# A hybrid decoder layer on one core: the first head's row maxima turned in the projection's stage and loaded with the queries, and a third score pass of 100 rows

## The chip, the core and the metric

The kernel is one launch on one core of a Trainium2 chip. The core has five engines with queues of their own: TensorE (PE, matmuls; PEld are its weight loads), VectorE (DVE), ScalarE (ACT), GpSimd (POOL) and SyncE (SP, which here issues nearly all DMAs). Each engine works through its instructions in order and waits at semaphores for the others. Operands lie in SBUF (128 partitions), matmul results in the eight banks of PSUM, the rest in DRAM. The metric is the device time of one execution in microseconds (us); the figure for a kernel is the median over its runs.

## The reference, cut to what matters

One layer over 1040 tokens (16 learned meta tokens ahead of 1024) of width 1024: a norm, one input projection to 7328 columns, four parallel mixers, each gated and projected back, and an output projection. The change touches the second mixer, attention with 8 heads of 96 query/key dimensions (64 plain and 32 rotary) and 64 value dimensions:

```python
z = rms_norm(h_res, pre_norm_g) @ w_in
(pv, pg, cq, ckv, kr, mg, cu, cg, sbcx, sg, gl) = split_cols(z)
q = (rms_norm(cq, q_norm_g) @ w_uq) ...      # 8 heads x 96, scaled by 96 ** -0.5
kv = (rms_norm(ckv, kv_norm_g) @ w_ukv) ...  # 8 heads x (64 of k, 64 of v)
s = where(k_pos <= q_pos, q @ k.T, -inf)     # causal
p = softmax(s)                               # needs the maximum of each row of s
o = p @ v
y_b = (o * silu(mg)) @ w_out_mla
```

All of it is in float32. The output is the 1024 rows that follow the meta tokens.

## The kernel before

**Stages.** The kernel runs in three stages. In the first (up to about 641 us) PE works through the input projection: pairs of 256-column chunks, each made of seven products of twelve matmuls each (128x512 most of them), into the banks ps_pa to ps_pd. The other parts (convolutions, norms, the queries and keys, and weights made ready for later) are written as Python generators, the lanes, which are advanced a step after each product. Results go to DRAM (z, th, q, k, kr, v). In the second stage (to about 841 us) PE does the attention, head by head and for each head two halves c of 512 queries, with the projections of the other mixers (ps_y) as fill. The third is the projection of attention's result and the output projection.

**Order.** No engine's order is written by hand. Every operation is recorded with its reads and writes (`Plan.record`), and `Plan.flush` then plays the recorded list through a rough model of the engines' times and issues the instructions in the order in which that model starts them. So an edit in one place can move instructions elsewhere. It flushes once per stage. All compute instructions are issued from one helper, so the profile calls them all L362, and they are told apart by their tiles. DMA completions of SP and ACT are counted on eight lanes (DMAHW0 to DMAHW7), which are given out in the order of issue: a DMA waits until the one eight places ahead of it has landed.

**Precision.** A float32 operand is split into a high part and the remainder (`split`), and a product is three matmuls: high x high, high x low, low x high. `q_dram` and `k_dram` hold both parts (index s of 0 and 1).

**Scores and their maxima.** For softmax the score tile is built keys by queries. Query tile `qt` and key tile `kt` have `NA = 100` partitions: 96 of data (`QK`) and four more. In the four extra rows of `kt` (high part) stands -1, loaded once from `ones_dram`; in the four extra rows of `qt` stands the row maximum of the query, each row r holding the maxima of the r-th 128 queries and zeros elsewhere. So the first of the three score passes, over 100 rows, subtracts each query's maximum within the matmul; the second and third are over 96 rows (`attend`, L1478 to L1481). Then DVE adds the causal mask on the diagonal block, ACT takes the exponential (tile p), ACT and POOL split it (tile pt), and three matmuls add it to ps_o.

**Where the maxima come from.** `row_maxima` computes scores queries by keys from the high parts alone (ps_x in the first stage, ps_s<-kt,qt in the second), masks them and reduces them on DVE to mx, and then to four columns of 128 maxima. For the first head (`h < FIRST`) this is done in the projection's stage by `task_first`, which leaves the four columns in `mrs`; for the others `maxima` does it in the attention stage, ahead of the half in which they are used. In both cases `maxima` then turns the four columns into rows: a transpose on PE (128x4 to 4x128, into a ps_s bank), and one DVE operation that multiplies it by the unit matrix into the four extra rows of `qt`.

**The switch from stage one to two.** The second stage's first loads are issued on SP while PE is still in the projection: `load_q(0, 0)`, the masks, the -1 rows and a zero fill of `vs`, then head 0's keys and values (`load_kv(0)`: kt<-k, kt<-kr twice, vs<-v three times, vt<-v), the queries of (0, 1) and (1, 0), and head 1's keys and values. The first head's first score matmul needs `qt` with its maxima and `kt`.

Of the kernel before, what the change touches and what calls it, by code (L numbers as in the profile page):

```python
# [21 lines left out]
F32 = mybir.dt.float32  # L22
F32R = mybir.dt.float32r
BF16 = mybir.dt.bfloat16
AF = mybir.ActivationFunctionType
ALU = mybir.AluOpType
AX = mybir.AxisListType
# [3 lines left out]
P = 128  # L31
# [3 lines left out]
L = NT + NM  # L35
# [7 lines left out]
QK = 96  # L43
# [7 lines left out]
FIRST = 1  # L51
# [21 lines left out]
def f(ap):  # L73
    return ap.bitcast(F32)
# [393 lines left out]
def trunk_kernel(ctx, tc, a):  # L468
    nc = tc.nc
    plan = Plan(nc)  # L470
    PE, ACT, DVE, POOL, SP = (plan.engine(e) for e in ("PE", "ACT", "DVE", "POOL", "SP"))
# [7 lines left out]
    def ld(out, in_):  # L479
        SP.dma_start(f(out) if out.dtype == F32R else out, f(in_) if in_.dtype == F32R else in_)  # L480
# [17 lines left out]
    const = pool(ctx, name="const")  # L498
    dram = pool(ctx, name="dram", space=DRAM)
    ident = const.pool.tile([P, P], F32, name="ident")  # L500
# [10 lines left out]

    par = const.tile([P, NPAR + 2], F32, name="par")

    mrs = const.tile([P, FIRST, 2, 4], F32, name="mrs")

    z_dram = {}
    for n in ("a0", "a1", "ckv", "kr", "pv0", "pv1", "c0", "c1", "x0", "x1"):
        z_dram[n] = dram.tile([P, L], F32, name=f"z_{n}")
# [15 lines left out]
    mask_dram = [dram.tile([P, P], F32, name=f"mask{i}") for i in range(2)]  # L534
    zero_dram = dram.tile([NS, 2 * P], F32, name="zero")
    ones_dram = dram.tile([4, L], F32, name="ones4")

    so_dram = [dram.tile([2, P, D], F32, name=f"so{k}") for k in range(KH)]

# [13 lines left out]
    def bank(tag="x"):  # L553

        return psum.tile([P, 512], F32, tag=tag, bufs=2 if tag == "x" else 1, name=f"ps_{tag}")
# [3 lines left out]
    tp = pool(one, name="tp", reuse_waits="tile")  # L559
# [3 lines left out]
    def t4(shape, dt=F32, name="t4"):  # L563
        return tp.tile(shape, dt, tag="t4", bufs=4, name=name)
# [398 lines left out]
    def task_consts():  # L963

        for i in range(2):
            mask = w1([P, P], name="mask")
            causal(mask, 1 - 2 * i)
            ld(mask_dram[i], mask)
        t = t4([4, L], name="kone")
        POOL.memset(t, -1.0)  # L970
        ld(ones_dram, t)
        t = t4([NS, 2 * P], name="zero")
        POOL.memset(t, 0.0)
        ld(zero_dram, t)
        yield

    def k_rows(k_, h, part):
# [7 lines left out]
    def row_maxima(c, mx, q_, k_, mask, bank):  # L985

        for r in range(4):
            nk = NM + P * (4 * c + r + 1)
            nb = -(-nk // 512)
            w_ = -(-nk // nb)  # L990
            w_ += w_ % 2
            n0 = 0
            for b in range(nb):
                n = min(w_, nk - n0)
                s = bank()
                PE.matmul(s[:, :n], q_[:, P * r:P * (r + 1)], k_[:, n0:n0 + n], start=True, stop=True)
                if b == nb - 1:
                    add(DVE, s[:, n - P:n], s[:, n - P:n], mask)
                DVE.tensor_reduce(mx[:, r, b:b + 1], s[:, :n], axis=AX.X, op=ALU.max)
                n0 += n  # L1000
            yield
# [206 lines left out]
    def task_first(c):  # L1208

        n = NM + 512 * (c + 1)  # L1210
        for h in range(FIRST):
            k_ = t4([QK, L], F32R, name="k0")[:, :n]
            k_rows(k_, h, lambda x: x[:, 0, :n])
            q_ = t4([QK, 512], F32R, name="q0")
            ld(q_, q_dram[c][h][:, 0])
            mask = w1([P, P], name="mask")
            causal(mask)
            yield
            mx = tp.tile([P, 4, 3], F32, name="mx")
            POOL.memset(mx, NEG)  # L1220
            yield from row_maxima(c, mx, q_, k_, mask, bank)
            DVE.tensor_reduce(mrs[:, h, c], mx, axis=AX.X, op=ALU.max)

    def task_kv():

# [179 lines left out]
    NA = QK + 4  # L1405
    qt = {}

    def load_q(h, c):
        qt[h, c] = qk.tile([NA, 2, 512], F32R, tag="q", bufs=3, name="qt")
        ld(qt[h, c][:QK].rearrange("p s n -> p (s n)"), q_dram[c][h].rearrange("p s n -> p (s n)"))  # L1410

    load_q(0, 0)
    kt = [qk.tile([NA, 2, LK], F32R, name=f"kt{i}") for i in range(2)]
# [7 lines left out]
    for t in vs:  # L1421
        ld(t.rearrange("p c n -> p (c n)"), zero_dram)
    for t, src in ((maskS, mask_dram[0]), (maskT, mask_dram[1]),
                   *((kt[i][QK:NA, 0, :L], ones_dram) for i in range(2))):
        ld(t, src)

    def load_kv(h):
# [15 lines left out]
    def maxima(h, c):  # L1443

        q_, k_ = qt[h, c], kt[h % 2]
        if h < FIRST:
            mr = mrs[:, h, c]  # L1450
            for _ in range(4):
                yield
        else:
            mx = mxs[:, h % 2, c]
            yield from row_maxima(c, mx, q_[:QK, 0], k_[:QK, 0], maskS, lambda: bank("s"))
            mr = at.tile([P, 4], F32, tag="mr", bufs=2, name="mr")
            DVE.tensor_reduce(mr, mx, axis=AX.X, op=ALU.max)
        pm = bank("s")
        PE.transpose(pm[:4, :P], mr, ident)
        DVE.tensor_tensor(q_[QK:NA, 0, :].rearrange("p (r n) -> p r n", n=P),  # L1460
                          pm[:4, :P].unsqueeze(1).to_broadcast([4, 4, P]),
                          ident[:4, :4].unsqueeze(2).to_broadcast([4, 4, P]), op=ALU.mult)
        yield
# [3 lines left out]
    def attend(h, c):  # L1467
# [4 lines left out]
        for j in range(nj):  # L1472
# [5 lines left out]
            s = bank("s")[:kn, :n]  # L1478
            PE.matmul(s, k_[:NA, 0, ks], q_[:NA, 0, qs], start=True, stop=False)
            PE.matmul(s, k_[:QK, 0, ks], q_[:QK, 1, qs], start=False, stop=False)  # L1480
            PE.matmul(s, k_[:QK, 1, ks], q_[:QK, 0, qs], start=False, stop=True)  # L1481
            d0 = P * j - NM
            dl, dh = max(d0, 512 * c, 0), min(d0 + P, 512 * (c + 1))
            if dh > dl:
# [407 lines left out]
```

## Time and profile before

| what | value |
|---|---|
| median of 3 runs | 974.67 us (974.61 to 975.8) |
| the profiled execution: its time | 973.71 us |
| the profiled execution: its span, first to last instruction | 971.8 us |
| granted TensorE clock | 0.998 |
| PE busy | 959.1 us, 99% of the span |
| DVE, POOL, ACT busy | 695.7, 672.1, 450.7 us |
| chain of work that ended last | PE 93%, DMA 2%, DVE 2%, POOL 2%, issue 1%, ACT 1% |

The span is 1.9 us shorter than the execution's time: what lies around the instructions. In the rows of the profile, "out<-in" names the tile written and the tiles read, without buffer numbers; qt, kt, ps_s, ps_o, p and pt are the tiles named above. An "idle before" in square brackets is time in which the engine had nothing to do just before, with what ended it. Matmuls overlap, so the distance from one start to the next is what a matmul costs on PE, and the printed duration is longer. A "q" behind an engine (SPq, ACTq) is its queue: here the issue of a DMA.

### The profile page before, as it was taken

How to read it: one execution, taken by the hardware profiler on the slowest of the kernel's cores; microseconds unless marked ns; L12 is line 12 of the kernel's file. 1: busy time of each engine (PE TensorE's matmuls, PEld its weight loads, DVE VectorE, ACT ScalarE, POOL GpSimd, SP SyncE). 2: the span in 40 equal slices, each digit the busy share in tenths (PEclk: the TensorE clock that was granted, in tenths of full speed). 3: DMA queues.
4: the chain of work that ended last, by engine and by line, in shares of the span. 5: the costliest groups of instructions: out<-in, count | busy, mean ns of one | idle time of the engine just before them, and what ended most of it. 6: DMA issues, size and time to landing. Idle time of an engine off the chain costs nothing.

```text
span 971.8 us, 15351 instructions
## 1 busy us (share of the span) xinstructions
PE 959.1 (99%) x5063; PEld 817.5 (84%) x5063; DVE 695.7 (72%) x1118; ACT 450.7 (46%) x914; POOL 672.1 (69%) x623
## 2 busy tenths in 40 slices
PE   9999999999999999999999999999999999999996
PEld 9999899889888888888778888878888888788885
DVE  6946967969978985435545687346768878699956
ACT  7644333343343454554443444356465565224632
POOL 6747645566677888888679689556377696557965
PEclk9999999999999999999999999999999999999999
DMA  7145467667587686685646778699869773772644
GB/s 257 35 115 167 143 228 235 218 202 243 183 283 245 188 277 202 214 264 177 218 148 184 245 264 276 187 306 332 227 180 280 188 209 120 265 252 85 203 150 152
DMA packets 136295, 202.76 MB, mean 209 GB/s; under 512 B 20814, under 2 KB 83253, under 8 KB 135448
## 3 DMA queue, kind: packets, MB, share of 16 engines
q1 hardware_dynamic: 127240, 185.00, 61.2%
q10 hardware_dynamic: 8656, 15.74, 4.5%
q0 software_dynamic: 320, 1.05, 0.3%
q8 instruction: 40, 0.66, 0.3%
q14 instruction: 39, 0.32, 0.1%
HBM read 128.86 MB, written 72.88 MB: 208 GB/s over the span
## 4 chain that ended last, share of the span: by engine, by line
PE 93%; DMA 2%; DVE 2%; POOL 2%; issue 1%; ACT 1%; DVEq 0%; SPq 0%; POOLq 0%; ACTq 0%
PE ps_pb L362 17%; PE ps_pa L362 16%; PE ps_pc L362 15%; PE ps_o L362 9%; PE ps_u L362 8%; PE ps_pd L362 7%; PE ps_y L362 7%; PE ps_s L362 7%; PE ps_x L362 5%; PE ps_w L362 1%; DMA kt<-k 1%; POOL pt L362 1%; DMA kt<-kr 1%; POOL boM L362 0%; ACT pt L362 0%
## 5 line engine op out<-in xcount | busy, mean ns | idle before, releaser
L362 PE MATMUL ps_pb<-T,S 128*128 128x512 f32 (+2 forms) x792 | 172.4, 360 | 0.0
L362 PE MATMUL ps_pa<-B,A 128*128 128x512 f32 (+2 forms) x792 | 169.4, 359 | 0.0
L362 POOL TENSOR_TENSOR S<-ss,S 128x512 fp32r<-128x512 f32 x84 | 114.0, 1370 | 64.5 <-ACT S L362 64.3
L362 PEld LDWEIGHTS ps_pa<-B,A 128*128 128x128 f32 x792 | 134.3, 188 | 22.5 <-issue 0.7
L362 PEld LDWEIGHTS ps_pb<-T,S 128*128 128x128 f32 x792 | 134.1, 189 | 22.4 <-issue 1.0
L362 POOL TENSOR_TENSOR A<-raw,A 128x512 fp32r<-128x512 f32 x84 | 114.7, 1371 | 42.8 <-ACT A L362 40.5
L362 POOL TENSOR_TENSOR pt<-p,pt 128x512 fp32r<-128x512 f32 (+1 forms) x96 | 101.1, 1077 | 53.7 <-PE ps_s L362 25.6
L362 DVE TENSOR_TENSOR u<-ps_pb,u 128x512 f32<-128x512 f32 (+2 forms) x66 | 40.2, 610 | 80.6 <-PE ps_pb L362 76.8
L362 ACT ACTIVATE S<-ss 128x512 fp32r<-128x512 f32 x84 | 50.8, 628 | 83.9 <-DVE ss L362 52.5
L362 DVE SCALAR_TENSOR_TENSOR ps_w<-conv,par,ps_w 128x512 f32<-128x512 f32 x116 | 87.2, 752 | 2.3
L362 PE MATMUL ps_y<-bo,whl 128*128 128x512 f32 x288 | 86.2, 405 | 0.4 <-DVE th L362 0.4
L362 PE MATMUL ps_pc<-B,S 128*128 128x512 f32 (+1 forms) x396 | 86.2, 360 | 0.0
L362 PE MATMUL ps_pd<-T,A 128*128 128x512 f32 (+2 forms) x396 | 85.4, 359 | 0.0
L362 PE MATMUL ps_pc<-T,S 128*128 128x512 f32 (+1 forms) x396 | 85.0, 358 | 0.0
L362 ACT ACTIVATE p<-ps_s 128x512 f32<-128x512 f32 (+4 forms) x112 | 49.5, 443 | 59.5 <-PE ps_s L362 29.7
L362 PEld LDWEIGHTS ps_pc<-B,S 128*128 128x128 f32 x396 | 66.9, 189 | 11.7 <-issue 1.2
L362 PEld LDWEIGHTS ps_pc<-T,S 128*128 128x128 f32 x396 | 66.9, 188 | 10.7
L362 PEld LDWEIGHTS ps_pd<-T,A 128*128 128x128 f32 x396 | 66.9, 189 | 10.4
L362 PE MATMUL ps_s<-qt,kt 100*128 100x512 f32 (+4 forms) x336 | 68.0, 325 | 1.3 <-DVE qt L362 1.3
L362 PE MATMUL ps_o<-pt,vt 128*128 128x512 f32 (+7 forms) x288 | 68.1, 345 | 0.8 <-ACT ol L362 0.6
L362 PEld LDWEIGHTS ps_s<-qt,kt 100*128 100x128 f32 (+1 forms) x336 | 54.3, 176 | 11.2 <-DVE qt L362 1.6
L362 DVE TENSOR_TENSOR z<-ps_pc,u 128x512 f32<-128x512 f32 (+1 forms) x64 | 38.8, 606 | 32.7 <-PE ps_pc L362 29.0
(280 smaller groups left out, 1917.8 us busy)
## 6 DMA issues: line engine op xcount, KB each, us to landing
raw<-in_w_in_dram SPq DMA_DIRECT2D x52, 512.0 KB
th<-th SPq DMA_DIRECT2D x32, 512.0 KB
th<-z ACTq DMA_DIRECT2D x60, 256.0 KB
v<-vhl SPq DMA_DIRECT2D x16, 384.0 KB
qt<-q SPq DMA_DIRECT2D x16, 384.0 KB
vt<-v SPq DMA_DIRECT2D x8, 768.0 KB
bo<-bo SPq DMA_DIRECT2D x6, 1024.0 KB
kt<-k SPq DMA_DIRECT2D x8, 520.0 KB
```

Source lines behind the costliest of these rows:

```text
L362: getattr(self.handle[o["eng"]], o["op"])(*map(real, o["args"]), **{k: real(v) for k, v in o["kw"].items()})
```

## The change

`task_first` no longer leaves its four columns in `mrs`. It transposes them itself in the projection's stage (into a ps_x bank), copies the 4x128 result over the first four partitions of its mask tile, and writes each of the four rows by a DMA of its own into a new DRAM tile `top_dram`, which was filled with zeros beforehand, so that it holds the four extra rows of `qt` as they are to stand. `load_q` of the first head gets a second DMA that loads these four rows. In `maxima` the transposes and the DVE products of the first head's two halves are gone. Apart from this, the third score pass takes in all 100 rows, for all heads: the four extra rows of `kt`'s low part are loaded once with zeros from another new DRAM tile, so that the result stays as it was.

```diff
-    mrs = const.tile([P, FIRST, 2, 4], F32, name="mrs")
...
+    none_dram = dram.tile([4, L], F32, name="ones4")
+    top_dram = dram.tile([4, 2, 4, P], F32, name="top")
...
+        t = t4([4, L], name="knone")
+        POOL.memset(t, 0.0)
+        ld(none_dram, t)
         t = t4([NS, 2 * P], name="zero")
         POOL.memset(t, 0.0)
         ld(zero_dram, t)
+        ld(top_dram.rearrange("r c (a b) n -> (r c a) (b n)", b=2), t[:16])
...
             yield from row_maxima(c, mx, q_, k_, mask, bank)
-            DVE.tensor_reduce(mrs[:, h, c], mx, axis=AX.X, op=ALU.max)
+            mr = tp.tile([P, 4], F32, name="mr")
+            DVE.tensor_reduce(mr, mx, axis=AX.X, op=ALU.max)
+            pm = bank()
+            PE.transpose(pm[:4, :P], mr, ident)
+            DVE.tensor_copy(mask[:4].bitcast(F32R), pm[:4, :P])
+            for r in range(4):
+                ld(top_dram[r:r + 1, c, r], mask[r:r + 1])
...
         ld(qt[h, c][:QK].rearrange("p s n -> p (s n)"), q_dram[c][h].rearrange("p s n -> p (s n)"))
+        if h < FIRST:
+            ld(f(qt[h, c])[QK:NA, 0], top_dram[:, c].rearrange("r a n -> r (a n)"))
...
-                   *((kt[i][QK:NA, 0, :L], ones_dram) for i in range(2))):
+                   *((kt[i][QK:NA, 0, :L], ones_dram) for i in range(2)),
+                   *((kt[i][QK:NA, 1, :L], none_dram) for i in range(2))):
         ld(t, src)
...
         if h < FIRST:
-            mr = mrs[:, h, c]
-            for _ in range(4):
+            for _ in range(5):
                 yield
-        else:
-            mx = mxs[:, h % 2, c]
-            yield from row_maxima(c, mx, q_[:QK, 0], k_[:QK, 0], maskS, lambda: bank("s"))
-            mr = at.tile([P, 4], F32, tag="mr", bufs=2, name="mr")
-            DVE.tensor_reduce(mr, mx, axis=AX.X, op=ALU.max)
+            return
+        mx = mxs[:, h % 2, c]
+        yield from row_maxima(c, mx, q_[:QK, 0], k_[:QK, 0], maskS, lambda: bank("s"))
+        mr = at.tile([P, 4], F32, tag="mr", bufs=2, name="mr")
+        DVE.tensor_reduce(mr, mx, axis=AX.X, op=ALU.max)
...
-            PE.matmul(s, k_[:QK, 1, ks], q_[:QK, 0, qs], start=False, stop=True)
+            PE.matmul(s, k_[:NA, 1, ks], q_[:NA, 0, qs], start=False, stop=True)
```

Instructions move at three places: the last 100 us of the projection, where the maxima are computed, the switch of stages, and the first 30 us of the attention. Ahead of the first and behind the last of them each engine's order is what it was.

PE at the switch, before. The rows run from the last product of the projection into the first half of head 0 (ps_s<-qt,kt: the score passes, three for each block of keys, kt_6897 being head 0's keys and kt_6903 head 1's; ps_s<-kt,qt: row maxima of head 1):

```order
L362 MATMUL ps_pc<-B_320,S_6687 128x512 x9
L362 MATMUL ps_s<-ident,mrs 4x128 x2
L362 MATMUL ps_s<-qt,kt_6897 128x512 [waits DMAHW3_49,DMAHW2_49,DMAHW5_49,DMAHW1_49,DVE_49]
L362 MATMUL ps_s<-qt,kt_6897 128x512 x2
...
L362 MATMUL ps_s<-qt,kt_6897 16x16 x2
L362 MATMUL ps_s<-kt_6903,qt 128x144 [waits DMAHW3_49,DMAHW2_49,DMAHW4_49,DMAHW1_49,Activation_49]
L362 MATMUL ps_o<-pt,vt_6911 128x512 [waits DMAHW7_49,Activation_49]
L362 MATMUL ps_s<-qt,kt_6897 128x512 [waits DMAHW0_49,Activation_49]
```

The same place after the change (kt_6922 is head 0's keys, kt_6924 head 1's):

```order
L362 MATMUL ps_pc<-B_320,S_6708 128x512 x9
L362 MATMUL ps_s<-qt,kt_6922 128x512 [waits DMAHW5_49,DMAHW6_49,DMAHW4_49,DMAHW7_49,DMAHW2_49,DMAHW0_49]
L362 MATMUL ps_s<-qt,kt_6922 128x512
L362 MATMUL ps_s<-qt,kt_6922 128x512 [waits DMAHW4_49]
...
L362 MATMUL ps_s<-qt,kt_6922 16x16 x2
L362 MATMUL ps_s<-qt,kt_6922 128x512 [waits DMAHW6_49,DMAHW5_49,Activation_49]
L362 MATMUL ps_s<-qt,kt_6922 128x512 x2
L362 MATMUL ps_o<-pt,vt_6934 128x512 [waits DMAHW4_49,Activation_49]
L362 MATMUL ps_s<-qt,kt_6922 128x512 [waits Activation_49]
...
L362 MATMUL ps_o<-pt,vt_6934 128x400
L362 MATMUL ps_s<-kt_6924,qt 128x144 [waits DMAHW2_49,DMAHW1_49,DMAHW7_49,DMAHW0_49,Activation_49]
```

The two transposes and the wait for DVE are gone from the first score matmul, which now waits for loads alone; three score matmuls of the second half stand ahead of the first ps_o, and head 1's first maxima stand eleven matmuls later.

SP at the switch, before: the second stage's loads, from the first head's queries to head 1's keys:

```order
L362 DMA qt<-q_4075 96x1024 [waits DMAHW2_49]
L362 DMA maskS<-mask_5675 128x128 [waits DMAHW3_49]
L362 DMA maskT<-mask_5777 128x128 [waits DMAHW4_49]
L362 DMA kt_6897<-ones_5875 4x1040 [waits DMAHW6_49,DMAHW5_49,DMAHW1_49]
L362 DMA vs_6899<-zero 80x256 [waits DMAHW0_49,DMAHW6_49,DVE_49,Pool_49]
L362 DMA vs_6901<-zero 80x256 [waits DMAHW7_49]
L362 DMA kt_6903<-ones_5875 4x1040 [waits DMAHW0_49,PE_49]
L362 DMA kt_6897<-k_1678 64x2x1040 [waits DMAHW1_49]
...
L362 DMA qt<-q_5254 96x1024 [waits DMAHW0_49]
L362 DMA qt<-q_4075 96x1024 [waits DMAHW1_49]
L362 DMA kt_6903<-k_1678 64x2x1040 [waits DMAHW2_49]
```

And after (qt<-top are the four rows of maxima; the kt<-ones_5885 are the zeros):

```order
L362 DMA qt<-top 4x512 [waits DMAHW5_49]
...
L362 DMA vs_6920<-zero 80x256 [waits DMAHW1_49,DMAHW2_49,DVE_49,Pool_49]
L362 DMA kt_6922<-ones_5872 4x1040 [waits DMAHW2_49]
L362 DMA kt_6924<-ones_5872 4x1040 [waits DMAHW3_49,PE_49]
L362 DMA kt_6922<-ones_5885 4x1040 [waits DMAHW4_49]
L362 DMA kt_6924<-ones_5885 4x1040 [waits DMAHW5_49]
L362 DMA kt_6922<-k_1678 64x2x1040 [waits DMAHW6_49]
...
L362 DMA qt<-q_5254 96x1024 [waits DMAHW5_49]
L362 DMA qt<-top 4x512 [waits DMAHW6_49]
L362 DMA qt<-q_4075 96x1024 [waits DMAHW7_49]
L362 DMA kt_6924<-k_1678 64x2x1040 [waits DMAHW0_49]
```

Three more small loads stand ahead of head 0's keys and four ahead of head 1's. The place eight behind the projection's last store from ACT (th<-z), which head 0's keys had, is now that of the second -1 rows, three places ahead of the keys.

PE in the projection after the change, where the first half's maxima end (ps_x<-k_5925,q_5944 are the row maxima, mr the four columns; T, B, S are operands of the projection). Before, the transpose's row was not there and the product ran on:

```order
L362 MATMUL ps_x<-k_5925,q_5944 128x264
L362 MATMUL ps_pb<-T_291,S_5932 128x512 x6
L362 MATMUL ps_x<-ident,mr 4x128
L362 MATMUL ps_pb<-T_291,S_5932 128x512
L362 MATMUL ps_x<-k_5950,q_5985 128x328
```

The transpose stands six matmuls behind the last of the scores whose maxima it turns; that of the second half stands seven behind.

## The prediction

> **What bounds the kernel now.** I read the page's first lines, then PE's waits, then stages, then the place of the one wait that the change removes.
>
> ```profile
> PE 959.1 (99%) x5063; PEld 817.5 (84%) x5063; DVE 695.7 (72%) x1118; ACT 450.7 (46%) x914; POOL 672.1 (69%) x623
> PE 93%; DMA 2%; DVE 2%; POOL 2%; issue 1%; ACT 1%; DVEq 0%; SPq 0%; POOLq 0%; ACTq 0%
> ```
>
> PE bounds the whole span: 959.1 of 971.8 us, and 93% of the chain that ended last. So only two things count: work put on PE or taken from it, and time in which PE stands. Of its waits, one stands at the place of the change:
>
> ```profile
> PE ps_s L362 <- DVE qt L362: 1.3, 1, 1.3
> ```
>
> It is one wait of 1.3 us for DVE's writing of `qt`. The windows round the switch of stages give its place (columns: busy time of PE, PEld, DVE, ACT, POOL with counts, clock, DMA share, GB/s):
>
> ```profile
> 627.00:641.00 14.00, 14.00 (x64) 11.48 (x63) 2.77 (x4) 2.14 (x3) 1.84 (x3) 1.00 1.03 221
> 641.00:645.00 4.00, 2.72 (x19) 2.16 (x17) 3.03 (x7) 1.73 (x3) 0.82 (x5) 1.00 1.02 324
> 645.00:655.00 10.00, 9.74 (x51) 7.97 (x51) 4.01 (x14) 9.48 (x22) 8.64 (x9) 1.00 1.02 370
> ```
>
> From 627 to 641 us PE is full; from 641 to 645 it loses 1.28 us, from 645 to 655 another 0.26. And the DMA engines are full from 627 to 655 us: whatever is loaded there queues. The timeline of the switch, all engines:
>
> ```profile
> 640.92 0.38 PE L362 MATMUL ps_s<-ident,mrs 128*4 128x128 f32 x2
> 641.12 0.69 DVE L362 TENSOR_TENSOR zlast<-ps_pc,u 128x512 f32<-128x512 f32 x1 [4.75 <-PE ps_pc L362]
> 641.84 1.28 DVE L362 TENSOR_TENSOR qt<-ps_s,ident 4x512 fp32r<-4x512 f32 x2
> 641.85 0.72 ACT L362 ACTIVATE zlast<-zlast,par 128x512 f32<-128x512 f32 x1 [2.70 <-DVE zlast L362]
> 642.58 2.27 PE L362 MATMUL ps_s<-qt,kt 100*128 100x512 f32 x15 [1.28 <-DVE qt L362]
> 643.96 0.60 ACT L362 ACTIVATE p<-ps_s 128x512 f32<-128x512 f32 x1 [1.39 <-DVE ps_s L362]
> 644.70 0.31 PE L362 MATMUL ps_s<-kt,qt 96*128 96x144 f32 x1
> 645.27 0.49 PE L362 MATMUL ps_o<-pt,vt 128*128 128x512 f32 x1 [0.26 <-ACT pt L362]
> ```
>
> PE ends the last product at 640.92 and does the two transposes. DVE must first drain the projection's last bank (641.12, 0.69 us) and only then writes `qt`; PE starts at 642.58. From 640.92 that is 1.66 us, of which the transposes hide 0.38.
>
> The chain of waits tells this otherwise, and must not be believed here:
>
> ```profile
> 623.62 2.10 DMA th<-z
> ...
> 625.73 0.54 SPq L362
> ...
> 626.33 5.82 DMA kt<-kr
> ...
> 632.16 9.64 DMA kt<-k
> ```
>
> It lays 9.64 us on head 1's keys (issued 632.16), up to DVE's qt. But DVE was in zlast until 641.12 + 0.69 = 641.81, and the first head's product needs nothing of head 1. That the load's end falls on the same time is chance. What the chain does show is when things land: the last ACT store at 625.72, and only then is head 0's kt<-k issued (it stands eight places behind that store); the first of its two kt<-kr lands at 632.15.
>
> **The change part by part.**
>
> *The wait.* 1.66 us between the last product and the first score go, if every load that the first score now waits for is there at 640.92. Gain 1.66.
>
> *Two transposes move into the projection*, where PE has no gap. In the first row above two of them last 0.38 together, and one alone lasts 0.27:
>
> ```profile
> L362 PE MATMUL ps_s<-ident,mrs x2: 271/272/272, 640.9 to 641.0; 128*4 128x128 f32 x2
> L362 DVE TENSOR_REDUCE mrs<-mx x2: 166/166/166, 550.4 to 565.2; 128x4 f32<-128x12 f32 x2
> L362 POOL MEMSET kone<- x1: 962/962/962, 529.6 to 529.6; 4x1040 f32 x1
> ```
>
> So each costs 0.11 of PE's stream: 0.2 us back. Do they make PE wait there? The first half's last score matmul and its reduction stand so:
>
> ```profile
> 549.31 0.28 PE L362 MATMUL ps_x<-k,q 96*128 96x264 f32 x1
> 553.39 2.88 PE L362 MATMUL ps_pd<-T,A 128*128 128x512 f32 x12
> 556.11 2.88 PE L362 MATMUL ps_pa<-B,A 128*128 128x512 f32 x12
> ```
>
> Twelve product matmuls take 556.11 - 553.39 = 2.72, one 0.227. `mrs` ended at 550.4 + 0.17, 1.3 us behind the score matmul's start; the new transpose stands behind that matmul (0.12) and six products (1.36), at 1.48. It fits by 0.2, so I take 0; a DVE that is late by one of its 0.69 us operations would cost up to 0.5, and the second half's transpose the same. DVE gets two copies of 4x128 in place of two 4x512 products (1.28 for both), and POOL a memset like kone's (0.96 us) in a stage where PE waits for neither.
>
> *What is late next.* With PE at 640.92 the first block's scores are ready for ACT 643.96 - 642.58 = 1.38 later, at 642.30. But ACT is in the projection's last tanh until 641.85 + 0.72 = 642.57, and only then starts p: 1.36 earlier than before, not 1.66. PE does not feel all of that, since three score matmuls of the second half (3 x 0.23) now stand ahead of the first ps_o; they need the bank that p frees at about 643.2, and PE, through its fifteen at 640.92 + 2.12 = 643.04, waits some 0.2 for it. Before, it stood 0.26 at this point. I charge 0.1, with bounds of -0.5 (the losses behind 642.58 vanish) and +0.3 (ACT's lateness comes through whole).
>
> *The loads.* SP issues three more small loads ahead of head 0's keys, and one more behind. Its rows at the switch:
>
> ```profile
> 623.36 0.27 SPq L362 DMA_DIRECT2D kt<-ones  x1
> 625.73 0.54 SPq L362 DMA_DIRECT2D kt<-k  x1
> ...
> 627.48 1.49 SPq L362 DMA_DIRECT2D vs<-v  x3
> ...
> 632.16 0.53 SPq L362 DMA_DIRECT2D kt<-k  x1
> ...
> 634.07 2.99 SPq L362 DMA_DIRECT2D vs<-v  x3
> 638.44 0.34 SPq L362 DMA_DIRECT2D vt<-v  x1
> ```
>
> The second -1 rows now stand eight behind the last ACT store and inherit its landing at 625.72; the two zero loads and kt<-k follow at some 0.35 each, so kt<-k goes out at about 626.8, 1.0 to 1.1 later. As the DMA engines are full from 627 on, all behind it lands about 1.1 later: head 0's first rotary rows (632.15 before) at 633.3, 7.6 ahead of 640.92. The cover is large: 0. Head 1's keys are closer. Before, PE used them at 644.70 with no gap, so they had landed by then; now by 645.8. The new order puts that maxima matmul eleven places later: 643.95 for the first ps_o (1.32 earlier than 645.27), then four score matmuls and three values with two short waits, about 646.0. The cover is 0.2: I take 0 and keep 0.5, later by 0.3.
>
> The projection's eight 512-byte stores and the two fills stand on SP among loads whose data PE uses many us later. For the nearest row: three small vs<-v take 1.49 of SP together, so eight take 4; 0 on the path.
>
> The Trainium skill, "DMA: Bandwidth & Descriptors", section "Anatomy of one DMA — SWDGE (gpsimd) path", speaks against so many small DMAs: about 2.0 us fixed for each, whatever its size. Paid one after another the four ahead of head 1's keys would be 8 us by that page, an estimate; the rows 627.48 (three in 1.49) show that issues overlap, and the sum goes by them. By that rule of the Trainium skill rival D, below, would be 8 instead of 5.8 us late.
>
> *The third pass over 100 rows.* Per head there are 5 and 9 blocks of keys, so 8 x 14 = 112 matmuls change their row count:
>
> ```profile
> L362 PE MATMUL ps_s<-qt,kt 96*128 96x512 f32 x96 | 31.2, 397 | 0.0
> L362 PE MATMUL ps_s<-qt,kt 100*128 100x512 f32 x48 | 19.3, 402 | 1.3 <-DVE qt L362 1.3
> L362 PEld LDWEIGHTS ps_s<-qt,kt 96*128 96x128 f32 x192 | 34.3, 190 | 4.7
> L362 PEld LDWEIGHTS ps_s<-qt,kt 100*128 100x128 f32 x96 | 18.0, 188 | 4.7 <-DVE qt L362 1.6 <-ACT p L362 0.2 <-DVE mxs L362 0.2
> ```
>
> 402 against 397 ns is a duration, not a distance, and the weight loads are 188 against 190: 0 of PE's stream. If the 5 ns were paid in full, 112 of them would be 0.6 us; I keep that in the range.
>
> *Sum.* 1.66 - 0.2 - 0.1 = 1.36, rounded to a gain of 1.3 us: against the profiled 973.71 (span 971.8 plus 1.9) it is 972.4. The median of the runs lies 0.96 above that execution, at 974.67, so the forecast there is 973.3. That is 0.14%; 0.2%, about what a measurement of this kernel can tell from no change, is 1.95 us.
>
> **The rivals.**
>
> *B: more is won.* The order of the first 25 us of the attention changes, and PE's losses behind the wait go with it: the start of the first ps_o is 0.57 behind the maxima matmul at 644.70, which needs 0.07 of PE, and at 645 to 655 the window shows 0.26 idle. With 0.5 and 0.26 added: 1.36 + 0.1 + 0.76 = 2.2, so 972.5. For it: ps_o no longer stands directly behind the first block. Against: ACT still sets the pace of these first units (9.48 of 10 us busy).
>
> *C: head 1's keys come late.* If they land at 647.0 instead of 645.8, PE waits 1.0 and keeps 0.3: 974.4. For it: full DMA engines and a cover of 0.2. Against: the few kilobytes added.
>
> *D: slower.* The small loads are not overlapped on a full queue. The rows from 634.07 are the pattern: three vs<-v and the start of vt<-v took 638.44 - 634.07 = 4.4 us, as each issue waited for the landing eight places ahead. Four such loads are 5.8 us, of which 1.1 is counted already: head 1's keys at 645.8 + 4.7 = 650.5, PE waits 4.5 at 646.0, and the time is 973.3 + 4.5 = 977.8. It decides for "slower" from a landing at 649.3 on (3.3 of waiting take 973.3 to 976.6). Against: those waits were for large loads ahead, which have to land anyway.
>
> *That the change doesn't do what it says* would show as a PE wait at 641 for another load; its cover is 7.6 us, and it has no chance of its own.
>
> **How the numbers follow.** The forecast has 0.46, B 0.32, C 0.11, D 0.11. B alone is faster by over 0.2%: 0.32. The forecast and C are within: 0.57. D is slower: 0.11. The predicted time is the forecast's, 973.3. The range holds the forecast's bounds (gains of 0.5 to 1.9, from 1.36 with the bounds above taken one or two at a time), B with another 0.6 below 972.5, and C with what 0.5 for a late transpose adds: 971.9 to 974.9. D is outside.
>
> **What would show it.** In the profile after: the first ps_s<-qt,kt directly behind the last ps_pc, with no 1.3 us wait for DVE qt; the first p on ACT at once behind zlast, 1.3 to 1.4 earlier relative to the last product; kt<-k of head 0 issued about 1 us later; no PE wait for DMA at the first ps_s<-kt,qt; the two ps_x<-ident,mr without idle before them; 100-row and 96-row passes at the same distances. The forecast is wrong if PE idles in 641 to 655 by more than 0.6 us, if the projection's end moves by more than 0.3 us, or if the third passes lengthen the stage.

## The result

| kernel | median | runs | ratio to before |
|---|---|---|---|
| before (measured again beside it) | 976.34 us (974.61 to 977.57) | 6 | |
| after | 981.73 us (980.11 to 984.42) | 6 | 1.0065, 95% interval 1.0048 to 1.0083 |

The change makes the kernel slower by 0.65%, some 5.4 us; forecast was a gain of 1.3. The profiled execution of the changed kernel is the slowest of its six (984.42 us, span 982.5), and that of the kernel before (973.71) lies below all six beside it, so the two traces are 10.7 us apart where the medians are 5.4 apart. The sizes below are those of the traces.

PE is still busy for nearly all of the span, but its share of the chain that ended last fell from 93% to 86%, and a load of keys has come into it with 3%. From the page of after:

```profile
PE 962.6 (98%) x5063; PEld 819.8 (83%) x5063; DVE 693.7 (71%) x1118; ACT 450.2 (46%) x914; POOL 673.8 (69%) x624
PE 86%; POOL 4%; DMA 4%; DVE 3%; issue 2%; ACT 1%; DVEq 0%; SPq 0%; POOLq 0%; ACTq 0%
```

PE's waits in the whole of after (us in total, times, longest):

```profile
PE ps_s L362 <- DMA kt<-k: 6.1, 2, 4.3
PE ps_w L362 <- POOL mhalf L362: 1.4, 1, 1.4
PE ps_o L362 <- ACT ol L362: 0.6, 1, 0.6
PE ps_s L362 <- DMA qt<-q: 0.5, 1, 0.5
```

The wait for DVE's `qt` is gone, and 6.1 us for keys have come. The switch of stages itself does what was forecast. Its timeline, PE in after:

```profile
639.21 2.88 PE L362 MATMUL ps_pc<-B,S 128*128 128x512 f32 x12
641.93 3.15 PE L362 MATMUL ps_s<-qt,kt 100*128 100x512 f32 x18
644.92 0.39 PE L362 MATMUL ps_o<-pt,vt 128*128 128x512 f32 x1
```

The first score follows the last product with no idle before it. The loss begins 25 us later. The chain of waits of after, rows between 640 and 700:

```profile
655.04 11.32 DMA kt<-k
666.49 0.47 PE ps_s L362 x2
...
677.96 14.87 DMA kt<-k
692.96 0.46 PE ps_s L362
...
693.87 4.47 PE ps_y L362 x10
```

Head 2's keys are asked for at 655.04 and land at 666.36; head 3's at 677.96 and land at 692.83. In the kernel before, the same loads went out here (SP's timeline):

```profile
656.11 0.52 SPq L362 DMA_DIRECT2D kt<-k  x1
...
675.55 0.52 SPq L362 DMA_DIRECT2D kt<-k  x1
```

and by the landing events of the trace landed at 662.42 and 687.07: 6.3 and 11.5 us, now 11.3 and 14.9. Head 1's values, some loads ahead of head 2's keys, were hardly late (648.91, 648.74 before); the last `th` ahead of these keys landed at 661.62 instead of 657.49. So the delay arises between the two, where the queries, two `bo` and the `th` are moved. In before the DMA engines had caught up at 655 to 658 us, just behind the rows that the prediction shows; in after they had not (windows of before, then of after; the last figures are the DMA engines' busy share and GB/s):

```profile
655.00:658.00 3.00, 3.00 (x19) 2.39 (x18) 2.58 (x8) 2.49 (x9) 3.00 (x4) 1.00 0.63 217
```

```profile
655.00:658.00 3.00, 2.90 (x15) 2.33 (x16) 2.12 (x5) 2.14 (x8) 3.00 (x4) 1.00 1.02 366
```

PE's timeline in after shows the two waits, and what comes behind the second:

```profile
666.49 0.47 PE L362 MATMUL ps_s<-kt,qt 96*128 96x144 f32 x2 [1.82 <-DMA kt<-k]
...
692.96 0.46 PE L362 MATMUL ps_s<-kt,qt 96*128 96x144 f32 x1 [4.29 <-DMA kt<-k]
...
693.72 4.61 PE L362 MATMUL ps_y<-bo,whl 128*128 128x512 f32 x10
```

The same ten ps_y in before:

```profile
687.60 2.55 PE L362 MATMUL ps_y<-bo,whl 128*128 128x512 f32 x10
```

The window of 690 to 700 of before (columns as in the prediction, the granted clock third from the end):

```profile
690.00:700.00 10.00, 10.00 (x54) 8.39 (x53) 7.63 (x21) 5.97 (x11) 5.08 (x4) 1.00 0.76 226
```

That of after, and the one behind it:

```profile
690.00:700.00 10.00, 7.04 (x23) 5.67 (x24) 3.69 (x10) 0.00 (x0) 0.00 (x0) 0.66 0.78 232
700.00:760.00 60.00, 60.00 (x316) 50.32 (x315) 45.48 (x111) 35.22 (x78) 38.62 (x38) 1.00 0.75 215
```

After 4.29 us without work the clock is at 0.66 on the mean of these 10 us, and ten products take 4.61 us instead of 2.55. From 700 on it is 1.00 again.

Where the 10.7 us come from is read from the end of each half of a head (PE's last ps_o of it), after minus before: -0.5 and -0.3 for the two halves of head 0, +1.8 and +1.5 for head 1, +6.1 for the first half of head 2, +8.6 for its second, then 8.6 through the next four halves, up to 757 us, 9.2 to 9.3 for the rest, 10.7 at the end. The last product already ends 1.0 us later in after, so the switch and head 0 win 1.5 and 1.4 us, and -0.5 and -0.3 are what is left of it. Then come 2 us for head 2's keys, whose maxima are worked out beside head 1; 4.5 for head 3's, likewise one head ahead; 2.5 at the low clock; 0.6 round 760; 1.5 in the last stage.

### The profile page after: what moved, and what is told of

It is laid out like the page before. It is cut to its first block, busy times and chain, and to the rows that moved or that the text cites. A ratio compares the mean times of both kernels' runs of the same rounds, so it can differ in the third digit from the quotient of the medians.

```text
span 982.5 us, 15357 instructions
## 1 busy us (share of the span) xinstructions
PE 962.6 (98%) x5063; PEld 819.8 (83%) x5063; DVE 693.7 (71%) x1118; ACT 450.2 (46%) x914; POOL 673.8 (69%) x624
## 4 chain that ended last, share of the span: by engine, by line
PE 86%; POOL 4%; DMA 4%; DVE 3%; issue 2%; ACT 1%; DVEq 0%; SPq 0%; POOLq 0%; ACTq 0%
PE ps_pa L362 16%; PE ps_pb L362 16%; PE ps_pc L362 15%; PE ps_pd L362 7%; PE ps_u L362 7%; PE ps_o L362 7%; PE ps_y L362 6%; PE ps_s L362 6%; PE ps_x L362 5%; DMA kt<-k 3%; DMA w_out_mla<-whl 1%; PE ps_w L362 1%; POOL pt L362 1%; DVE c L362 1%; DVE u L362 0%
## 5 line engine op out<-in xcount | busy, mean ns | idle before, releaser
L362 PE MATMUL ps_y<-bo,whl 128*128 128x512 f32 x288 | 88.3, 415 | 0.3 <-DVE th L362 0.3
L362 PEld LDWEIGHTS ps_pc<-B,S 128*128 128x128 f32 x396 | 66.9, 189 | 11.5 <-issue 1.0
L362 PEld LDWEIGHTS ps_pc<-T,S 128*128 128x128 f32 x396 | 66.9, 189 | 10.7 <-issue 0.2
L362 ACT ACTIVATE A<-raw 128x512 fp32r<-128x512 f32 x84 | 51.9, 626 | 24.0 <-PE ps_pd L362 8.8
```

The costliest lines, as they stand in the source:

```text
L362: getattr(self.handle[o["eng"]], o["op"])(*map(real, o["args"]), **{k: real(v) for k, v in o["kw"].items()})
```

## The experiments

Theory T, the first: the new small loads and the later start of the queue make the keys late. Its rivals: P, the removed `mrs` moves the attention's tiles in SBUF; O, one place of SP's order, left out of the forecast. Before: head 1's second queries `qt<-q` (96 rows), then the two `bo` loads (128 rows, 1 MB each). After, SP's timeline:

```profile
640.91 0.34 SPq L362 DMA_DIRECT2D bo<-bo  x1
644.13 0.33 SPq L362 DMA_DIRECT2D qt<-q  x1
644.51 0.42 SPq L362 DMA_DIRECT2D bo<-bo  x1
```

The queries wait for their buffer, and the first `bo` now goes ahead of them.

**Parts of the change, and the places in SBUF.**

```diff
 e1: the kernel before
+    none_dram ..., its zeros, kt[i][QK:NA, 1, :L] <- none_dram
-            PE.matmul(s, k_[:QK, 1, ks], q_[:QK, 0, qs], start=False, stop=True)
+            PE.matmul(s, k_[:NA, 1, ks], q_[:NA, 0, qs], start=False, stop=True)
 e2: the changed kernel with these lines taken back
 e3: the changed kernel
-                   *((kt[i][QK:NA, 0, :L], ones_dram) for i in range(2)),
-                   *((kt[i][QK:NA, 1, :L], none_dram) for i in range(2))):
+    POOL.memset(f(kt[i][QK:NA, 0, :L]), -1.0), POOL.memset(f(kt[i][QK:NA, 1, :L]), 0.0)
 e4: the changed kernel
+    pad = const.tile([P, FIRST, 2, 4], F32, name="pad")
+    POOL.memset(pad, 0.0)
```

> The kernel before with one part of the change alone: the third score pass over 100 rows, with the zero rows loaded into both key buffers (two more small loads ahead of head 0's keys). Theory T, late loads: two more loads on the sync engine move head 0's keys back by about 0.7 us (after: 627.70 against 625.73), the DMA queue stays full past the time at which head 2's keys are asked for, and those and head 3's land some us late: PE waits 1 to 5 us for kt<-k between 655 and 695 and the time is 0.2% to 0.5% over the kernel before. Rival P, places in SBUF (the removed tile moves the attention's tiles by 256 bytes): the tile is still there, so no wait for kt<-k and a ratio of 1.000. Rival O, the order of the second query load of head 1 against the first bo load: here that order is as before, so 1.000. Rival M, the 100-row pass itself costs matmul time: 112 matmuls, at most 0.6 us, ratio up to 1.0006, spread over the stage.

> The changed kernel without the 100-row third pass: no zero rows, no load of them, third pass over 96 rows as before; the transposes in the projection, the stores and the loads of the maxima stay. Theory T: two loads fewer ahead of head 0's keys than in the changed kernel, one more than before, so the keys go out about 0.7 us earlier than there; the waits for kt<-k shrink to 0 to 3 us, ratio 0.998 to 1.003. Rival P: the attention's tiles lie where the changed kernel has them, so the full loss: PE waits about 6 us for kt<-k, ratio 1.0065. Rival O: the order of those two loads is as before here, ratio 0.998 to 0.999.

> The changed kernel with the rows of -1 and of zeros written in place by GpSimd (four fills of 4x1040) instead of loaded: four small loads fewer ahead of the keys than in the changed kernel. Theory T: head 0's keys go out at about 626.3 instead of 627.7 or earlier, the queue drains as it did before, the waits for kt<-k go (under 1 us in all) and the granted clock stays at 1.00 in 690 to 700; what is won at the first score stays: ratio 0.998 to 1.000. Rival P: tiles lie as in the changed kernel, so ratio 1.0065 with 6 us of waits for kt<-k. Rival O: order as before, ratio 0.998 to 0.999, whenever the keys go out.

> The changed kernel with an unused tile of the size of the removed one in its place, so that every tile of the attention lies where it lay in the kernel before; the order of instructions is that of the changed kernel. Theory T: nothing changes, ratio 1.005 to 1.008, PE waits about 6 us for kt<-k. Rival P: the loss goes, ratio 0.998 to 1.000, no waits for kt<-k. Rival O: 1.0065, as the changed kernel.

Measured: e1 978.46 us, 1.0026 (1.0012 to 1.0039); e2 978.91, 1.0033 (1.0008 to 1.0058); e3 983.37, 1.0070 (1.0044 to 1.0096); e4 982.34, 1.0059 (1.0027 to 1.0090).

P falls: in e4 the tiles lie as before, and the waits are those of after:

```profile
PE ps_s L362 <- DMA kt<-k: 6.8, 2, 4.4
```

e3 was a miss. The four fills stand on POOL behind its last stores of the projection and ran only at 644.1 us (POOL's timeline of e3), so PE, which had ended the last product at 641.44, waited at the switch (its timeline):

```profile
644.10 3.68 POOL L362 MEMSET kt<- 4x1040 f32 x4
```

```profile
644.18 1.55 PE L362 MATMUL ps_s<-kt,qt 96*128 96x144 f32 x5 [2.74 <-DMA kt<-kr]
646.37 5.39 PE L362 MATMUL ps_s<-qt,kt 100*128 100x512 f32 x18 [0.64 <-POOL kt L362]
```

It says nothing on T. e2 is telling: its first score starts at 639.97, 2.6 us earlier than before, and its first half of head 0 ends 2.4 us earlier; yet head 2's and head 3's keys land at 662.73 and 688.20, no earlier than in before, and 3.9 us of waits for kt<-k take the gain and more. What PE wins at 641 it has to hand back at the next loads. The time of e2 lies just above the range of T (to 1.003); the values that P and O gave lie outside its interval.

**How much is queued ahead of the keys.** On SP the 2 MB of `bo` for the next branch stand ahead of head 3's keys.

```diff
 e5: the changed kernel; e6: the kernel before; e8: e2
-                if d == 4 and bi < 2:
+                if d == 6 and bi < 2:
                     with plan.behind():
                         load_bo(bi + 1)
 e7: the kernel before
             load_bo(0)
+            ld(bos[0, 1][:, 0], bo_dram[1][:, 0])
```

> The changed kernel with the two bo loads of each next branch (2 MB) asked for two output blocks later, which puts them behind head 3's keys and values on the sync engine instead of ahead of them. Theory T (now: from 627 to about 690 us the DMA engines are the bound, and the time follows the landing of head 3's keys, 687.1 before and 692.8 after the change): these keys have 2 MB less ahead of them, some 5 us at 400 GB/s, and land by 688; the 4.3 us wait for kt<-k and the low clock of 690 to 700 behind it go, head 2's wait of about 2 us stays; 5 to 7 us under the changed kernel, ratio to before 0.998 to 1.001. Rival S (the order in which wide and narrow loads mix makes the DMA engines lose their step, whatever is queued): no change, ratio 1.005 to 1.008.

> The same move of the bo loads in the kernel before. Theory T: head 3's keys landed at 687.07 and their first use started at 687.21, so the landing was just in time there; with 2 MB less ahead they land some 4 us earlier, and nothing waits for them: little to win in the runs where nothing waited, 1 to 3 us in the others; ratio 0.997 to 1.000. Rival S: 1.000. If the moved loads are late for their own products, slower.

> The kernel before with 512 KB more to load in this stage: half of the second bo tile is loaded a second time, behind head 2's keys and ahead of head 3's. Theory T: no slack, so head 3's keys land 1.3 us later, at about 688.4, PE waits 1 to 2 us for them, and the time is 0.1% to 0.3% longer (more, to 0.5%, if the wait is long enough to lower the clock). A rival in which the DMA engines have slack here, since PE hardly waits for a load in the kernel before: 1.000.

> The changed kernel without the 100-row third pass, and with the bo loads behind head 3's keys. Theory T: in the run without this move its first score came at 639.97 (642.58 before) and its span was still 3 us longer, as the keys of heads 2 and 3 came no earlier; with the move only head 2's wait of some 0.7 us is left and the gain is kept: ratio 0.996 to 0.999, faster than the kernel before. Rival S: as without the move, 1.001 to 1.006.

Measured: e5 976.28 us, 1.0013 (0.9996 to 1.0031); e6 976.21, 1.0014 (1.0003 to 1.0026); e7 977.28, 1.0021 (1.0008 to 1.0034); e8 974.31, 0.9994 (0.9980 to 1.0008).

At head 3's keys the DMA engines are the bound. Taking 2 MB from the front of these keys wins most of the loss back (e5), and 512 KB more in the kernel before, where PE hardly waited for a load, cost 0.21% (e7). PE's timeline of e7 has the wait at head 3's keys, as expected; it is put down to DVE, but the keys landed at 688.16, 0.13 ahead of its end:

```profile
688.29 0.31 PE L362 MATMUL ps_s<-kt,qt 96*128 96x144 f32 x1 [1.12 <-DVE ps_s L362]
```

In e5, head 2's wait stays, as expected (its waits):

```profile
PE ps_s L362 <- DMA kt<-k: 1.8, 1, 1.8
PE ps_y L362 <- DVE th L362: 1.7, 1, 1.7
```

The second row is a wait near 825 us that before and after do not have; it comes with another order of the later products, and e1, e6 and e8 have it too. So this way of moving the loads moves more than the loads. e5, e6 and e8 all lie a little above the ranges expected; e6, the move in the kernel before, is slower than before though no key comes late, which neither T nor S foresaw. g5, g7 and g8 below repeat the move with the loads alone.

**Small loads, and a first look at O.**

```diff
 f1: e1 with the third pass over k_[:QK, 1, ks], q_[:QK, 0, qs] again
 f2: e2 with
+                if d == (6, 4, 4)[bi] and bi < 2:
 f3: the changed kernel
-        while count["f"] < min(48, 48 * count["u"] / (NUNIT - 2)):
+        while count["f"] < min(48, 48 * (count["u"] - 1) / (NUNIT - 2 - 1)):
 f4: e5; ahead of load_kv(0) only kt[0][QK:NA, 0, :L] <- ones_dram is left
     load_kv(0)
+    three loads: the zeros of kt[0], the -1 rows and the zeros of kt[1]
```

> The kernel before with the zero rows loaded into both key buffers (two small loads ahead of head 0's keys) and nothing else: the third pass stays over 96 rows, so the rows loaded are never read. Its partner with the 100-row pass as well was 1.0026 of the kernel before. Theory T (two loads push the keys back in a stage bound by DMA): as that partner, 1.001 to 1.004, with head 3's keys landing at about 688. Rival M (the four rows more cost TensorE time): 1.000.

> The changed kernel without the 100-row pass, with the bo loads behind head 3's keys for the first branch alone; the second branch's go out where they did. The same with both moved was 0.9994 of the kernel before and had a wait of 1.7 us for th at 824 us. Theory T: the keys of heads 2 and 3 land as there, the loads after 700 us are as in the kernel before: 0.997 to 1.000. If the wait at 824 comes from the moved second branch, it goes, and 1 to 1.7 us with it.

> The changed kernel with the product work that fills the attention started one step later, which alone puts head 1's second query load back ahead of the first bo load, as in the kernel before. Rival O (that order makes the DMA engines lose their step, so that head 2's keys come 4 us late): head 2's keys land at 664 instead of 666.4, the wait at 666 shrinks from 1.8 to under 0.5, and the time falls 2 to 5 us under the changed kernel, ratio 1.001 to 1.004. Theory T (only what is queued ahead of the keys counts, and when the queue starts): as the changed kernel, 1.005 to 1.008.

> The whole change with the bo loads behind head 3's keys (1.0013 of before as it was) and with three of the four small loads of rows moved behind head 0's keys and values; only head 0's row of -1 stays ahead. Theory T: head 0's keys go out about 1 us earlier, at 626.1 instead of 627.1, and all loads behind head 1's go out as before, since three small loads still stand ahead of them: 0 to 1 us won, ratio 0.9995 to 1.0015. If the time hangs on the start of the queue alone: 0.999. If on the number of small loads alone: 1.0013.

Measured: f1 977.87 us, 1.0025 (1.0009 to 1.0042); f2 976.06, 1.0000 (0.9983 to 1.0016); f3 994.66, 1.0195 (1.0172 to 1.0218); f4 977.21, 1.0009 (0.9994 to 1.0024).

f1 costs what e1 costs, so the 100-row pass is free (in the traces e1 stays 0.8 us behind f1 from head 2 to the last head) and the two loads are not. But they do not cost through the keys: they land at 662.50 and 687.02, as in before. f1's waits are others, from another order further on:

```profile
PE ps_y L362 <- DVE th L362: 1.7, 1, 1.7
PE ps_s L362 <- DVE qt L362: 1.5, 2, 1.3
PE ps_w L362 <- POOL mhalf L362: 1.4, 1, 1.4
PE ps_o L362 <- ACT ol L362: 1.4, 2, 1.0
```

f2 has the th wait of 1.7 as well, so that doesn't come from the second branch's move. f3 shifted the whole filling with products and is no test of time; yet head 2's keys landed at 662.83, in the old order. f4's time lies in the range of T, but its trace speaks against T: head 0's keys go out at 625.66, as in before, and head 2's land at 665.40 all the same. By then head 2's keys had landed at 662.0 to 663.6 in the nine kernels with the old order (e3, late from the start, left out), and at 665.4 to 667.0 in the four with the new one.

**The two orders by hand.** To change SP's order alone, single loads are moved in the finished order; every other row stays.

```diff
+        for late, firsts in self.moves:
+            moved = [o for o in order if o["i"] in late]
+            order = [o for o in order if o["i"] not in late]
+            k = max((j for j, o in enumerate(order) if o["i"] in firsts), default=0)
+            order[k + 1:k + 1] = moved
         for o in order:
             self.issue(o)
 g3: the kernel before, (1, 1)'s queries behind the first bo
 g6: the changed kernel, the first bo behind (1, 1)'s queries
 g5: the kernel before, the next branch's two bo behind head 3's values
 g7: the changed kernel, with g5's move; g8: e2 with g5's move
 g4: the changed kernel, with g6's and g5's moves
```

> The kernel before with one thing moved: on the sync engine, head 1's second query load (96 rows) stands behind the first of the two bo loads (128 rows, 1 MB each) instead of ahead of both, as in the changed kernel. Nothing else changes in any engine's order of tiles. Theory O (this order is what makes head 2's keys late): head 2's keys land at about 666 instead of 662.4, head 3's at 691 or later instead of 687.1, PE waits 3 to 7 us for kt<-k and its clock falls behind it; ratio 1.003 to 1.008. Theory T (the small loads and the late start of the queue are): no change, 1.000, with the keys at 662 and 687.

> The changed kernel with these two loads put back in their old order on the sync engine and nothing else changed. Theory O: head 2's keys land at 663, head 3's at 687 to 688, the 6 us of waits for kt<-k shrink to 1 to 2, the clock stays up; 4 to 6 us under the changed kernel, ratio to before 0.999 to 1.002. Theory T: the loads still start late, so 1.005 to 1.008.

> The changed kernel with two moves on the sync engine alone: head 1's second query load ahead of the first bo load, and the two bo loads of the next branch behind head 3's keys and values. Theory O with the DMA engines as the bound: waits for kt<-k under 1 us in all, and the 1.66 us of the first score are kept: 0.997 to 0.9995, faster than the kernel before. Theory T: the second move alone works, as 1.0013 before.

> The changed kernel without the 100-row pass (its second query load already stands ahead of the bo loads), with the bo loads of the next branch behind head 3's keys and values on the sync engine and nothing else moved. The same without the move was 1.0033 with 3.9 us of waits for kt<-k. Theory O with the DMA engines as the bound: head 3's keys land by 683, only some 0.7 us of wait for head 2's keys is left: 0.997 to 0.9995. If a load that is moved back is late for its own product: 1.000 or more.

> The kernel before with the two bo loads of the next branch moved behind head 3's keys and values on the sync engine, and nothing else. With this move and the swap the changed kernel was 0.9968 of the kernel before. If that gain is the change's own, shown once the keys come in time, the move alone brings little here, where head 3's keys landed just in time in the profiled execution: 0.9985 to 1.000. If the gain is the move's, whatever the change: 0.996 to 0.998.

> The changed kernel with the same move and nothing else; the query load still stands behind the first bo load. If the two causes add (order of the query load: head 2's keys; 2 MB ahead of head 3's keys): head 2's keys land at 666 and PE waits 1.8 us there, head 3's by 684 with no wait and the clock stays up; 0.999 to 1.001, between 1.0040 (swap alone) and 0.9968 (both). If the query load's order alone mattered: 1.004 to 1.0065.

Measured: g3 978.62 us, g6 980.68, g4 973.84, g8 977.00, g5 974.43, g7 973.95. Landings are by the events of each profile:

| kernel | queries, first bo | next two bo | head 1's values land | head 2's keys | head 3's keys | PE waits for kt<-k | ratio (95%) |
|---|---|---|---|---|---|---|---|
| before | old | ahead | 648.74 | 662.42 | 687.07 | 0 | |
| g3 | new | ahead | 649.32 | 666.06 | 691.05 | 3.3 | 1.0019 (0.9993 to 1.0045) |
| after | new | ahead | 648.91 | 666.36 | 692.83 | 6.1 | 1.0065 (1.0048 to 1.0083) |
| g6 | old | ahead | 648.20 | 664.13 | 689.23 | 3.6 | 1.0040 (1.0015 to 1.0064) |
| g7 | new | behind | 646.53 | 662.58 | 679.59 | 0 | 0.9982 (0.9960 to 1.0005) |
| g4 | old | behind | 647.21 | 662.51 | 679.36 | 0 | 0.9968 (0.9945 to 0.9992) |
| g5, before | old | behind | 646.37 | 662.02 | 681.10 | 0 | 0.9986 (0.9964 to 1.0008) |
| g8, e2 | old | behind | 648.70 | 663.81 | 683.00 | 0.7 | 1.0001 (0.9977 to 1.0025) |

g3 shows O in the trace: one load moved in the kernel before, and head 2's keys land 3.6 us later, head 3's 4.0. Its windows of 641 to 665 beside before's (before first, g3 second; the last figures are the DMA engines' busy share and GB/s):

```profile
641.00:665.00 24.00, 22.47 (x130) 18.88 (x129) 14.83 (x42) 18.46 (x44) 17.07 (x24) 1.00 0.97 320
```

```profile
641.00:665.00 24.00, 22.12 (x127) 18.34 (x125) 14.45 (x41) 18.41 (x44) 16.67 (x23) 1.00 1.01 288
```

The engines are no less busy and move 10% less. After moves 291 there, g6 323. These are single executions, and before has the shortest way to its keys of all. In time, g3's 0.19% can't be told from nothing, where 0.3% to 0.8% was expected; the waits in its trace, PE's timeline:

```profile
666.20 0.30 PE L362 MATMUL ps_s<-kt,qt 96*128 96x144 f32 x1 [1.11 <-DMA kt<-k]
691.19 0.30 PE L362 MATMUL ps_s<-kt,qt 96*128 96x144 f32 x1 [2.21 <-DMA kt<-k]
```

The order is not all, however. g6, with the old order, was to be at 0.999 to 1.002 and keeps 0.40%, and g7, with the new one, lands head 2's keys at 662.58, where 666 was expected; its queue was 2.4 us ahead of after's when head 1's values landed, though its edit changes nothing so early: executions differ by as much. From these values to head 2's keys it took 13.7 to 15.9 us in the thirteen profiles of the old order (again without e3) and 16.1 to 17.9 in the six of the new, 15.3 and 17.0 on the mean. In all nineteen the keys land 4.2 to 5.2 us behind the last `th`; the difference arises ahead of it. The order costs some 1.8 us of landing; whether PE feels them hangs on how far the queue happens to be.

The 2 MB ahead of head 3's keys decide more: 0.7% from g6 to g4, which were measured together, and 0.8% from after to g7, which were not. With both moves the changed kernel (g4, 973.84 us) is the fastest, and the only one whose interval lies below 1. How much of that is the change's own can't be told: the kernel before with the same move (g5) is at 0.9986, and the intervals overlap. g8, with the same two orders but without the 100-row pass and its zero loads, was expected at 0.997 to 0.9995 and is at 1.0001. A gain of the change itself is not shown.

## Why the prediction was wrong

*The wait* was right: it went, and the score starts behind the product. *Two transposes move into the projection* was right within the spread: no wait for them, and the last product ends at 640.1 to 642.1 (mean 641.16) in the thirteen profiles with them, at 640.9 to 641.6 (mean 641.23) in the seven without. After's 642.10 broke the 0.3 us that the prediction set, but 0.8 of its 1.0 had come by 445 us, ahead of any moved instruction. *The third pass over 100 rows* was right: 0, by f1 against e1, and by the offset of 8.6 us that the next four halves of heads leave as it is. *What is late next* was right: head 0's two halves win 1.5 and 1.4 us against the projection's end, and the sum gave 1.36.

*The loads* is the step that failed, where it took 0. Up to head 1's keys it was right: head 0's keys go out at 627.70, or 626.7 with the projection's 1.0 us taken off (626.8 was forecast), and head 1's land at 643.52 without a wait of PE. It stopped there, with DMA engines that its own window showed full to the end of its rows. It left out that a queue still full at the next keys makes PE hand back what it has won (e2), and that one query load had changed places with 1 MB (g3: 3.6 us later keys). In place of the 0 stand 6.1 us of waits and 2.5 at a low clock. The small loads ahead of the keys had moved head 1's values by 0.2 us only; what they add behind that, and why g6 with the old order still loses 0.40%, stays open.

Rival D had the sign (977.8, against 981.73 measured) with another cause: its wait was to be at head 1's keys, for loads that are not overlapped; that its sign came true is luck. Rival C named the right resource, one head too early. No case went past head 1.

## What to carry to other kernels

Where the DMA engines are full, a gain on the compute engine lasts only to the next load it needs: follow the queue to the first point at which it runs dry, and price each load there by its landing, not by its issue. A wait of some us for data can cost half as much again in clock (4.3 and 2.5 us here). When a planner sets the order, compare the order of the DMA queue over all of the full stretch: two loads that changed places made the next keys some 1.8 us later, and 2 MB ahead of the keys weighed more here than the instructions that the change was about. With these loads moved the changed kernel no longer loses (0.9982 and 0.9968 instead of 1.0065).

## What was not expected of the hardware

The length of a pause alone does not say whether the clock falls. The ten ps_y behind head 3's keys take 2.53 us in e2 after 3.21 us of idling, 3.72 in g6 after 2.91, 3.97 in g3 after 2.21. PE's timelines of e2, g6 and g3:

```profile
688.33 0.30 PE L362 MATMUL ps_s<-kt,qt 96*128 96x144 f32 x1 [3.21 <-DMA kt<-k]
...
688.73 2.53 PE L362 MATMUL ps_y<-bo,whl 128*128 128x512 f32 x10
```

```profile
689.37 0.46 PE L362 MATMUL ps_s<-kt,qt 96*128 96x144 f32 x1 [2.91 <-DMA kt<-k]
...
690.12 3.72 PE L362 MATMUL ps_y<-bo,whl 128*128 128x512 f32 x10
```

```profile
691.58 3.97 PE L362 MATMUL ps_y<-bo,whl 128*128 128x512 f32 x10
```

The traces' clock shows what does. In all twenty profiles the granted clock changes only at points that lie a whole number of 3.413 us apart, and what counts is how much of one such step PE idles. In g3 the pause lies within one step, 1.2 us of 3.4 are busy, and the next step is at half clock; in e2 a border at 686.8 splits the longer pause, each step keeps 1.75 us or more of work, and the clock stays (windows along these steps, g3 first, then e2):

```profile
688.89:692.30 3.41, 1.20 (x8) 1.06 (x8) 2.50 (x7) 0.00 (x0) 0.00 (x0) 1.00 1.01 279
692.30:695.72 3.42, 3.42 (x10) 2.49 (x10) 0.69 (x1) 0.00 (x0) 0.00 (x0) 0.51 0.60 183
```

```profile
683.37:686.79 3.42, 1.75 (x10) 1.29 (x9) 2.44 (x6) 0.98 (x5) 0.70 (x2) 1.00 1.03 219
686.79:690.20 3.41, 1.87 (x11) 1.65 (x12) 0.77 (x4) 0.00 (x0) 0.00 (x0) 1.00 0.88 285
```

From 8 to 960 us of the twenty profiles, all eight steps at full clock in which PE idles 1.9 us or more are followed by half clock; of eleven with 1.4 to 1.8 three are, and of all those with less, one. The Trainium skill, "TensorE: Matmul & The Clock Gate", section "What's actually happening", gives a free-running window of about 3.4 us and half the clock after an idle one. The traces agree on the window and on the half; that a window needs to be idle throughout does not hold here (2.21 of 3.41 us were enough), and the measurement decides.

The keys' load moves less than the loads around it. In before, `bo` (128 rows) fills 650 to 652, and head 2's keys (64 rows) most of 658 to 662:

```profile
650.00:652.00 2.00, 2.00 (x11) 1.63 (x10) 1.05 (x4) 1.94 (x5) 1.71 (x2) 1.00 1.04 426
...
658.00:660.00 2.00, 2.00 (x15) 1.95 (x14) 0.31 (x2) 1.48 (x4) 0.82 (x4) 1.00 1.05 228
660.00:662.00 2.00, 2.00 (x14) 1.77 (x13) 1.97 (x6) 1.51 (x4) 1.73 (x2) 1.00 1.00 200
```

All three show full engines, at 426, 228 and 200 GB/s. The length of the packets is not the reason: in the trace the keys' packets of 4160 bytes take some 0.33 us each, those of 4096 bytes of `th` at 655 us 0.16. That the 64 rows are the reason was not tested. In g3, 660 to 662 moves 147. Why a 96-row load between two of 128 rows lowers the rate of what follows was not settled; that the parts of a load then finish further apart (the last `th` ahead of head 2's keys: 1.7 us in before, 4.5 in g3, by its landing events) is what the trace shows of it.
